# Moving a ring of matmul operands and the first loads of the down projection, in a two-layer encoder kernel

## The chip, the cores and the metric

One core of one Trainium2 chip runs the whole program. The metric is the device time of one execution in microseconds (us), the median of several executions. The engines are named as the profile names them: PE (TensorE matmuls), PEld (its weight loads), DVE (VectorE), ACT (ScalarE), POOL (GpSimd) and SP, which here only issues DMAs.

## The reference

Two layers, each a token mixer (first latent attention, then differential attention) and a SwiGLU feed-forward part, with a layer norm after each. The change touches the feed-forward part alone, which runs once in each layer:

```python
D_MODEL = 1024; SEQ = 1024; DEPTH = 2
D_FF = -(-8 * D_MODEL // (3 * 256)) * 256          # 2816
def _swiglu(x, w_gu, w_down):
    gate, up = jnp.split(x @ w_gu, 2, axis=-1)
    return (jax.nn.silu(gate) * up) @ w_down
...
h = _layernorm(ALPHA * h + _swiglu(h, ffn_w_gu[i], ffn_w_down[i]), ln_ffn_g[i], ln_ffn_b[i])
```

All data are float32.

## The kernel before, in words

**Precision.** A float32 product is made of three matmuls of rounded operands. `split` (L478) makes the two parts of an operand: the rounded high part `hi` is a cast on ACT (L480), the rest `lo` is a subtraction on DVE or POOL (L481). `op_unit` (L485) takes a place for such a pair from a ring of buffers: tags `wh` and `wl` have three places each, tag `o` has six.

**The gate and up stage** has 22 units of hidden columns. Each unit takes seven products of a Strassen-like scheme, called 1, 6, 2, 7, 5, 4, 3 in that order, each of 12 matmuls (`product`, L526). Their other operands are kept in SBUF: x itself, `t2` for product 6, `t3` for 7, `t1` for 5, `t4` for 4, `b22` for 3. `gr` is the raw weight tile of a unit; DVE makes its sums at L557 to L565 before the operands are split. DVE takes the products out of PSUM (L605 to L617), ACT does the silu (L628), DVE multiplies (L632, L633) into `hp`, POOL makes four further combinations `sh` of two units (L637 to L640), and SP stores both to `h_dr` in DRAM. The first two units of a layer have fewer products left, since part of them was made earlier; `stream` is the list of (unit, product) in which the products are asked for.

**The down stage** has seven passes of 11 units, each unit 12 matmuls (`step`, L795). The first pass, accumulator `dx`, multiplies `op_h_1_j` (from the loads `rh_1_0`, `rh_1_1`, `rh_1_2`, which hold units 0 to 3, 4 to 7 and 8 to 10 of `h_dr`) with `op_w_b_j` (printed in full `op_w_b11_j`, from the loads `tt_j` of the down weights). The second, `dy`, multiplies `op_h_5_j` with `op_w_t_j`, which is made from `tt_j` after its first half was replaced by a difference (the subtraction in `t1()`, L763). The `lo` parts of `op_h` are made on DVE, those of `op_w_b` on POOL, but on DVE for the first `early` units. The ring `o` of the down stage lies in the pool `fd`, which is opened where the gate stage's operands lay.

**Order.** A scheduler walks the program and its own costs and writes one order for each engine; `high_priority` and `behind(a, b)` (a stays behind b) steer it. On the chip each engine then runs its list strictly in order, so an instruction that waits holds back all that stands behind it on its engine. The same holds for SP's list of DMAs.

Of the kernel before, what the change touches and what calls it, by code (L numbers as in the profile page):

```python
# [16 lines left out]
P = 128  # L17
# [11 lines left out]
NFF = DFF // P  # L29
# [13 lines left out]
def trunk(  # L43
# [33 lines left out]
    V, A, G, T = nc.vector, nc.scalar, nc.gpsimd, nc.tensor  # L77
# [399 lines left out]

    def split(dst, src, eng):  # L478
        hi, lo = dst
        A.copy(hi, src)  # L480
        return eng.tensor_tensor(lo, src, f32(hi), ALU.subtract).ins  # L481

    turns = {"op": 0}

    def op_unit(src, eng, name, tags=("wh", "wl"), pool=None):  # L485

        tag = tags[turns["op"] % len(tags)]
        turns["op"] += 1
        where = wp if tag in ("wh", "wl") else pool
        t = where.tile([P, 2, 512], F32R, tag=tag, name=f"op_{name}", bufs=6 if pool is where else 3)  # L490
        turns["last"] = split((t[:, 0], t[:, 1]), src, eng)
        return t

    def swap(side):
        return "left" if side == "right" else "right"

    def ffn(side, xo, xst, pending, layer, x_src, x_dst, lng, lnb, next_x, spare=()):
# [5 lines left out]
        h_dr = [dr.tile([7, P, 4, 512], F32, name=f"h_dr{layer}_{g}") for g in range(3)]  # L503
        xst[2].close()
        st = ExitStack()
        pool = st.enter_context(tc.tile_pool(name=f"ff{layer}", bufs=1, side=side, reuse_waits="tile"))
        pool4 = st.enter_context(tc.tile_pool(name=f"ft{layer}", bufs=1, side=swap(side), reuse_waits="tile"))
        pool_a = xst[3]

# [2 lines left out]
        npre = 6  # L512
# [32 lines left out]
        begun = set()  # L545
# [79 lines left out]

        def activations(n, u2, u3, p1, g0):
            j, kh = n // 2, n % 2
            A.activation(u2, u2, AF.Silu)  # L628
            if kh == 0:
                hp[j] = big_tile(f"hp{layer}_{j}", F32).rearrange("p a (b c) -> p (a b) c", b=2)  # L630

            V.tensor_tensor(hp[j][:, kh], g0, p1, ALU.mult)  # L632
            V.tensor_tensor(hp[j][:, 3 - kh], u2, u3, ALU.mult)  # L633
            if kh:
                h11, h12, h22, h21 = (hp[j][:, i] for i in range(4))
                t = big_tile(f"sh{layer}_{j}", F32).rearrange("p a (b c) -> p (a b) c", b=2)
# [25 lines left out]

        r11, r12, r21, r22 = (xo["r", k, t] for k, t in ((0, 0), (0, 1), (1, 0), (1, 1)))
        xs = {}
        for key, where in (("t2", pool), ("t1", pool), ("b22", pool), ("t3", pool), ("t4", pool4)):
            xs[key] = [
                where.tile([P, 4, 512], F32R, tag=f"{key}{p}", name=f"{key}{p}_{nm}") for p in "hl"
            ]
# [1 line left out]
        def part(key, k, src, eng):  # L670
            split([t[:, k] for t in xs[key]], src[:, k], eng)

        stream = [(n, pr) for n in range(2) for pr in "53"]
        for n in range(NFF):
            stream += [(n, pr) for pr in ("674" if n < 2 else "67543" if n < npre else "1627543")]
        ahead = 4

        for k in range(4):
# [27 lines left out]
        for i in (1, 0):  # L706
            xst[i].close()
        st = ExitStack()
        pool = st.enter_context(tc.tile_pool(name=f"fd{layer}", bufs=1, side=side, reuse_waits="tile"))
        stx = ExitStack()  # L710
        poolh = stx.enter_context(tc.tile_pool(name=f"fh{layer}", bufs=2, side=swap(side), reuse_waits="tile"))
        poolx = stx.enter_context(tc.tile_pool(name=f"fx{layer}", bufs=1, side=swap(side), reuse_waits="tile"))
# [3 lines left out]
        tags = ("wh", "o", "wl", "o")  # L716

        tt = {
            j: poolx.tile([P, 2, 512], F32, tag=f"tt{j}", name=f"tt{layer}_{j}")
            for j in (range(11) if swap(side) == "left" else reversed(range(11)))  # L720
        }

        chain, in_order, banks_read = [], [], []

        def load_down(dst, src):

            i = nc.sync.dma_start(dst, src).ins
            if in_order:
                behind(i, chain[-1])
            chain.append(i)  # L730

        def from_h(s, name, tags=tags, late=False):

            for gi, (j0, j1) in enumerate(groups):
                r = poolh.tile([P, 4, 512], F32, tag="rawh", name=f"rh{layer}_{name}_{gi}")
                load_down(r[:, :j1 - j0], h_dr[gi][s, :, :j1 - j0, :])
                for j in range(j0, j1):
                    t = op_unit(r[:, j - j0], V, f"h{layer}_{name}_{j}", tags, pool)
                    if late and j > 1:
                        behind(turns["last"], banks_read[-1])  # L740
                    yield t

        def w_block(kh, cs, name):
# [6 lines left out]
                    yield r[:, j - j0]  # L750

        def unit(src, name, eng=G, tags=tags):
            return op_unit(src, eng, f"w{layer}_{name}", tags, pool)


        def b11():
            for j in range(11):
                load_down(tt[j], w_dn[layer, j].rearrange("p (b c) -> p b c", b=2))
                yield unit(tt[j][:, 0], f"b11_{j}", V if j < early else G)

        def t1():
# [18 lines left out]
        def t4():  # L780
            for j, r in enumerate(w_block(1, lo_half, "t4")):
                i = V.tensor_tensor(r, r, tt[j][:, 0], ALU.subtract).ins
                if j > 1:
                    behind(i, banks_read[-1])
                if next_x is not None:
                    yield unit(r, f"t4_{j}", G, ("o",))
                    continue
                t = poolx.tile([P, 2, 512], F32R, tag=f"tt{j}", name=f"wt4{layer}_{j}")
                split((t[:, 0], t[:, 1]), r, G)
                yield t  # L790

# [48 lines left out]
        hs = from_h(3, "5")  # L840
# [658 lines left out]
```

## Time and profile before

| quantity | value |
|---|---|
| median of 3 executions | 2296.66 us (2295.4 to 2297.1) |
| the profiled execution's own time | 2296.31 us |
| its span in the trace | 2294.4 us |
| PE busy | 2249.9 us, 98% of the span |
| DVE, ACT, POOL busy | 1562.8, 1017.9, 864.8 us |
| mean granted clock of PE | 0.995 of full speed |
| DMA moved | 288.28 MB, mean 126 GB/s |

PE is busy nearly all the time, so what counts are the short stretches in which it waits. The execution outside the span takes 2296.31 - 2294.4 = 1.9 us. The profile's waits name for each idle stretch of an engine the instruction that ended it; its timeline gives each instruction with its start.

### The profile page before, as it was taken

What the parts mean: (1) busy time and instruction counts of PE and PEld (TensorE: products, weight loads), DVE (VectorE), ACT (ScalarE), POOL (GpSimd) and SP (SyncE); (2) the same over time, 40 slices, a digit from 0 to 9 for tenths busy, and PEclk for the clock granted to TensorE, in tenths of its full rate; (3) what the DMA queues carried; (4) which work ended last, traced back from release to release, by engine and by line L of the source; (5) the groups of instructions that cost most, each with busy time, mean ns of one, the idle gap of its engine ahead of it and who ended that gap; (6) DMA issues with size and microseconds to landing.
All of it is one profiled execution on the core that took longest, in us unless ns stands there. A gap on an engine that the chain in (4) does not pass through costs nothing.

```text
span 2294.4 us, 31183 instructions
## 1 busy us (share of the span) xinstructions
PE 2249.9 (98%) x11410; PEld 1915.7 (83%) x11410; DVE 1562.8 (68%) x2899; ACT 1017.9 (44%) x2096; POOL 864.8 (38%) x688
## 2 busy tenths in 40 slices
PE   8999999999999999999999999999999999999997
PEld 8899997878888887888888888987778888887886
DVE  5667664696666668667476667676677666658777
ACT  4455573342333334445465656555432233324353
POOL 2232241114444445555432424221014444436564
PEclk9999999999999999999999999999999999999999
DMA  5010125334435338454310212054244232337353
GB/s 201 14 34 31 41 72 181 136 130 145 177 132 198 125 114 326 184 188 156 102 47 24 66 37 70 19 211 144 96 170 154 72 125 82 130 123 304 141 205 121
DMA packets 105545, 288.28 MB, mean 126 GB/s; under 512 B 7968, under 2 KB 30112, under 8 KB 94896
## 3 DMA queue, kind: packets, MB, share of 16 engines
q1 hardware_dynamic: 100976, 275.87, 33.6%
q0 software_dynamic: 4416, 10.42, 1.6%
q8 instruction: 90, 1.47, 0.3%
q14 instruction: 63, 0.52, 0.1%
HBM read 205.00 MB, written 77.07 MB: 123 GB/s over the span
## 4 chain that ended last, share of the span: by engine, by line
PE 88%; DVE 6%; DMA 3%; issue 2%; ACT 1%; POOL 1%; SPq 0%; DVEq 0%; POOLq 0%; ACTq 0%
PE gb L526 14%; PE gc L526 10%; PE ga L526 10%; PE dw L795 6%; PE zp_a L394 4%; PE s_a L216 4%; PE s_b L216 3%; PE dx L795 3%; PE dv L795 3%; PE bp L143 3%; PE bp L144 3%; PE bp L145 3%; PE dy L795 3%; PE o_a L255 2%; PE o_b L255 2%
## 5 line engine op out<-in xcount | busy, mean ns | idle before, releaser
L480 ACT CAST op_g<-gr 128x512 fp32r<-128x512 f32 x240 | 146.9, 621 | 370.8 <-PE gb L526 183.3
L481 POOL TENSOR_TENSOR op_g<-gr,op_g 128x512 fp32r<-128x512 f32 x104 | 146.4, 1413 | 248.2 <-ACT op_g L480 142.7
L481 DVE TENSOR_TENSOR op_h<-rh,op_h 128x512 fp32r<-128x512 f32 x154 | 163.8, 1091 | 63.4 <-ACT op_h L480 63.4
L526 PE MATMUL ga<-xh_m,op_g 128*128 128x512 f32 x512 | 168.1, 389 | 0.0
L480 ACT CAST op_h<-rh 128x512 fp32r<-128x512 f32 x154 | 92.9, 619 | 136.6 <-PE dx L795 36.1
L795 PE MATMUL dw<-op_w_t,op_h 128*128 128x512 f32 x660 | 151.4, 390 | 0.1
L795 PEld LDWEIGHTS dw<-op_w_t,op_h 128*128 128x128 f32 x660 | 123.6, 188 | 26.0 <-DVE op_h L481 0.5
L222 ACT ACTIVATE l_b<-l_b,mx_b 128x256 f32<-128x256 f32 (+7 forms) x128 | 99.5, 778 | 79.7 <-DVE mx_b L219 77.6
L1303 POOL TENSOR_SCALAR l_b<-l_b,r_b,cst 128x128 f32<-128x128 f32 (+3 forms) x64 | 52.8, 825 | 204.6 <-DVE r_b L224 194.0
L795 PE MATMUL dx<-op_w_b,op_h 128*128 128x512 f32 x528 | 122.2, 391 | 6.8 <-ACT op_w_b L480 3.9
L481 POOL TENSOR_TENSOR op_w_t<-tt,op_w_t 128x512 fp32r<-128x512 f32 x66 | 98.6, 1497 | 79.6 <-ACT op_w_t L480 77.8
L795 PEld LDWEIGHTS dx<-op_w_b,op_h 128*128 128x128 f32 x528 | 98.6, 188 | 30.1 <-ACT op_w_b L480 4.7
L481 DVE TENSOR_TENSOR op_g<-gr,op_g 128x512 fp32r<-128x512 f32 x136 | 110.8, 819 | 15.6 <-ACT op_g L480 15.3
L526 PE MATMUL gb<-t4h_f,op_g 128*128 128x512 f32 x352 | 115.9, 390 | 3.4 <-DVE tmp L609 3.4
L481 POOL TENSOR_TENSOR op_g<-s,op_g 128x512 fp32r<-128x512 f32 x40 | 54.3, 1358 | 167.9 <-ACT op_g L480 159.6
L526 PE MATMUL gb<-t2h_f,op_g 128*128 128x512 f32 x352 | 115.6, 390 | 0.4 <-DVE op_g L481 0.4
L526 PE MATMUL gc<-t1h_f,op_g 128*128 128x512 f32 x352 | 115.4, 389 | 0.0
L526 PE MATMUL gc<-b22h_f,op_g 128*128 128x512 f32 x352 | 115.3, 389 | 0.0
L526 PE MATMUL gb<-t3h_f,op_g 128*128 128x512 f32 x352 | 115.2, 389 | 0.0
L526 PEld LDWEIGHTS ga<-xh_m,op_g 128*128 128x128 f32 x512 | 96.1, 188 | 19.9
L143 PE MATMUL bp<-xT_f,h_wb 128*128 128x512 f32 x256 | 103.0, 402 | 0.0
L145 PE MATMUL bp<-xT_f,l_wb 128*128 128x512 f32 x256 | 101.6, 397 | 0.0
(378 smaller groups left out, 6753.9 us busy)
## 6 DMA issues: line engine op xcount, KB each, us to landing
gr<-in_w_gu SPq DMA_DIRECT2D x44, 1024.0 KB, 6.9
rh<-h_dr SPq DMA_DIRECT2D x28, 1024.0 KB, 4.8
h_dr<-sh SPq DMA_DIRECT2D x22, 1024.0 KB, 5.1
h_dr<-hp SPq DMA_DIRECT2D x22, 768.0 KB, 4.1
tt<-in_w_dn SPq DMA_DIRECT2D x22, 512.0 KB, 7.9
rh<-h_dr SPq DMA_DIRECT2D x14, 768.0 KB, 4.3
wo_dr<-op_pwo SPq DMA_DIRECT2D x16, 512.0 KB, 3.4
z<-xs_dr SPq DMA_DIRECT2D x16, 512.0 KB, 10.0
```

The costliest lines, as they stand in the source:

```text
L143: T.matmul(ps_out, lh, rh, start=(i == 0), stop=False)
L144: T.matmul(ps_out, lh, rl, start=False, stop=False)
L145: T.matmul(ps_out, ll, rh, start=False, stop=(i == n - 1))
L216: T.matmul(s[:, :w], lh, rh[:, ks], start=(j == 0), stop=(j == len(q_pass) - 1))
L222: A.activation(l[:, :n], l[:, :n], AF.Exp, bias=mx, scale=-1.0, accum_out=sm)
L255: T.matmul(po[:, c], a, b[:, j % 2, c], start=st, stop=sp_, skip_group_check=True)
L394: T.matmul(m, a[:, h, :], self.wo[h][w][:, c], start=(start and h == heads[0] and a is oh and w == 0), stop=(stop and h == heads[-1] and a ...
L480: A.copy(hi, src)
L481: return eng.tensor_tensor(lo, src, f32(hi), ALU.subtract).ins
L526: T.matmul(o, w[:, a, kc], x[b][:, k, :], start=(first and k == 0 and (a, b) == (0, 0)), stop=(k == 3 and a == 1), skip_group_check=True,)
L795: T.matmul(o, h[:, a, c], w[:, b_], start=(first and (a, b_) == (0, 0)), stop=(last and a == 1), skip_group_check=True,)
L1303: G.tensor_scalar(l1[:, :n], l1[:, :n], r1, nlam, ALU.mult, ALU.mult)
```

## The change

It does five things, in both layers.

- **Pools.** The gate stage's pool is cut in two (`t1`, `b22` in one, `t2`, `t3` in the other), and the down stage's pool too (results `z` and the norm's rows `g`, `b` in one, the ring `o` in the other), so that the ring `o` now lies under `t2` and `t3`, which the last gate unit reads earlier than `b22`. The tiles `tt` 0 to 3 get a pool apart from `tt` 4 to 10.
- **First four units of the down stage.** `early` goes from 3 to 4, h and w operands are asked for alternately, and the one load `rh_1_0` of 1 MB becomes four loads of 256 KB, one for each unit, put alternately with the loads of `tt_0` to `tt_3`.
- **`behind_gates`.** The casts of units 2 and 3 stay behind the last silu on ACT, and their subtractions behind the last `hp` product on DVE.
- **The subtractions of `t1()`.** That of unit j stays behind the `lo` part of `op_h_1_k`, k = min(j + 6, 10).
- **`stream`.** Products 6, 7 and 4 of the first two gate units alternate between the units: 6, 6, 7, 7, 4, 4.

```diff
     def split(dst, src, eng):
         hi, lo = dst
-        A.copy(hi, src)
+        turns["cast"] = A.copy(hi, src).ins
...
-        stream = [(n, pr) for n in range(2) for pr in "53"]
-        for n in range(NFF):
-            stream += [(n, pr) for pr in ("674" if n < 2 else "67543" if n < npre else "1627543")]
+
+        stream = [(n, pr) for n in range(2) for pr in "53"] + [(n, pr) for pr in "674" for n in range(2)]
+        for n in range(2, NFF):
+            stream += [(n, pr) for pr in ("67543" if n < npre else "1627543")]
...
-        for key, where in (("t2", pool), ("t1", pool), ("b22", pool), ("t3", pool), ("t4", pool4)):
+        for key, where in (("t1", pool), ("b22", pool), ("t2", pool2), ("t3", pool2), ("t4", pool4)):
...
-        pool = st.enter_context(tc.tile_pool(name=f"fd{layer}", bufs=1, side=side, reuse_waits="tile"))
+        pool, pool_o = [
+            st.enter_context(tc.tile_pool(name=f"f{n}{layer}", bufs=1, side=side, reuse_waits="tile")) for n in "do"
+        ]
...
+        def behind_gates():
+
+            behind(turns["cast"], turns["silu"])
+            behind(turns["last"], turns["hp"])
...
-                load_down(r[:, :j1 - j0], h_dr[gi][s, :, :j1 - j0, :])
+                one_by_one = name == "1" and gi == 0
+                if not one_by_one:
+                    load_down(r[:, :j1 - j0], h_dr[gi][s, :, :j1 - j0, :])
                 for j in range(j0, j1):
-                    t = op_unit(r[:, j - j0], V, f"h{layer}_{name}_{j}", tags, pool)
+                    if one_by_one:
+                        load_down(r[:, j - j0], h_dr[gi][s, :, j - j0, :])
+                    t = op_unit(r[:, j - j0], V, f"h{layer}_{name}_{j}", tags, pool_o)
                     if late and j > 1:
                         behind(turns["last"], banks_read[-1])
+                    if name == "1" and j > 1:
+                        behind_gates()
+                    splits.append(turns["last"])
                     yield t
...
-                V.tensor_tensor(tt[j][:, 0], tt[j][:, 1], tt[j][:, 0], ALU.subtract)
+                i = V.tensor_tensor(tt[j][:, 0], tt[j][:, 1], tt[j][:, 0], ALU.subtract).ins
+                behind(i, splits[min(j + 6, 10)])
...
-        early = 3
...
         with tc.high_priority(100):
-            hs, ws = (itertools.chain([next(x) for _ in range(early)], x) for x in (hs, ws))
+            begun = [[next(x) for x in (hs, ws)] for _ in range(early)]
+        hs, ws = (itertools.chain(b, x) for b, x in zip(zip(*begun), (hs, ws)))
```

The amount of work on PE, DVE and ACT hardly changes; the places change. Three of them follow, of layer 0. Lines of the changed kernel are shifted: its L560, L562, L564, L568, L608, L610, L612, L614 are L557, L559, L561, L565, L605, L607, L609, L611 of before; L738 is L727, L789 is L763, L645 and L646 are L642 and L643.

**First gate units, DVE.** `tmp_0` and `tmp_1` collect the products of units 0 and 1, and the L609 row reads product 7 of unit 0 out of PSUM (`gb_0`). Before:

```order
L605 TENSOR_TENSOR tmp_0_5697<-pg_0_5315,gb_0_5696 128x512
L481 TENSOR_TENSOR op_g_2_6_5734<-gr_2_5575,op_g_2_6_5734 128x512
L607 TENSOR_TENSOR tmp_0_5697<-tmp_0_5697,gc_05_5628 128x512
L557 TENSOR_TENSOR gr_4_5730<-gr_4_5730 128x512
L607 TENSOR_TENSOR tmp_0_5697<-tmp_0_5697,gc_03_5646 128x512
L605 TENSOR_TENSOR tmp_1_5760<-pg_0_5315,gb_1_5759 128x512
L559 TENSOR_TENSOR gr_4_5730<-gr_4_5730 128x512
L607 TENSOR_TENSOR tmp_1_5760<-tmp_1_5760,gc_15_5662 128x512
L561 TENSOR_TENSOR gr_4_5730<-gr_4_5730 128x512
L565 TENSOR_TENSOR s_0_4_5954<-gr_4_5730 128x512
L607 TENSOR_TENSOR tmp_1_5760<-tmp_1_5760,gc_13_5678 128x512
L609 TENSOR_TENSOR tmp_0_5697<-pg_0_5315,gb_0_5696 128x512
```

The same place in the changed kernel:

```order
L608 TENSOR_TENSOR tmp_0_5700<-pg_0_5318,gb_0_5699 128x512
L560 TENSOR_TENSOR gr_3_5601<-gr_3_5601 128x512
L481 TENSOR_TENSOR op_g_2_6_5740<-gr_2_5578,op_g_2_6_5740 128x512
L610 TENSOR_TENSOR tmp_0_5700<-tmp_0_5700,gc_05_5631 128x512
L562 TENSOR_TENSOR gr_3_5601<-gr_3_5601 128x512
L610 TENSOR_TENSOR tmp_0_5700<-tmp_0_5700,gc_03_5647 128x512
L608 TENSOR_TENSOR tmp_1_5720<-pg_0_5318,gb_1_5719 128x512
L568 TENSOR_TENSOR s_0_3_5862<-gr_3_5601 128x512
L564 TENSOR_TENSOR gr_3_5601<-gr_3_5601 128x512
L560 TENSOR_TENSOR gr_4_5736<-gr_4_5736 128x512
L610 TENSOR_TENSOR tmp_1_5720<-tmp_1_5720,gc_15_5665 128x512
L612 TENSOR_TENSOR tmp_0_5700<-pg_0_5318,gb_0_5699 128x512
```

Ten rows stand between the first and the last in both. The four on `gr_4`, of which the first needs a load, were among them, and now only the first of these is; three on `gr_3` have come in. In layer 1 no row on `gr_3` comes in and the last two on `gr_4` go behind the L612 row, so that eight are left. On PE, product 4 of unit 0, which writes the same PSUM bank `gb_0`, has two matmuls of unit 2 ahead of it that stood behind it before, in both layers.

**End of the gate stage, PE.** `gc_215` is product 3 of the last unit, the one that reads `b22`; `dx` is the first pass of the down stage. Before:

```order
L526 MATMUL gb_21_8271<-t4h_f_5485,op_g_21_4_8268 128x512
L526 MATMUL gc_215_8315<-b22h_f_5481,op_g_21_3_8286 128x512
...
L526 MATMUL gc_215_8315<-b22h_f_5481,op_g_21_3_8286 128x512
L795 MATMUL dx_0_8416<-op_w_b_0_8405,op_h_1_0_8395 128x512
L795 MATMUL dx_1_8417<-op_w_b_0_8405,op_h_1_0_8395 128x512
```

In the changed kernel:

```order
L529 MATMUL gb_21_8274<-t4h_f_5488,op_g_21_4_8271 128x512
L822 MATMUL dx_0_8436<-op_w_b_0_8409,op_h_1_0_8405 128x512
...
L822 MATMUL dx_3_8439<-op_w_b_0_8409,op_h_1_0_8405 128x512
L529 MATMUL gc_215_8318<-b22h_f_5482,op_g_21_3_8289 128x512
...
L529 MATMUL gc_215_8318<-b22h_f_5482,op_g_21_3_8289 128x512
L822 MATMUL dx_3_8439<-op_w_b_0_8409,op_h_1_0_8405 128x512
L822 MATMUL dx_0_8436<-op_w_b_1_8417,op_h_1_1_8413 128x512 x3
```

Eleven of the twelve matmuls of down unit 0 now run ahead of the last gate product (12 matmuls). In layer 1 unit 0 stands around product 4, and the first two matmuls of unit 1 ahead of the last gate product too. On SP the loads of unit 0 to 3 now stand in pairs, and those of `tt_3` and `rh_1_1` ahead of the store of the last `hp`; the load of the last three h units, `rh_1_2`, stands behind the same stores and the same eleven `tt` loads as before, and now directly behind the store of `sh_10`, which stood ahead of `tt_8` to `tt_10`.

**DVE at the eighth h unit.** `op_h_1_8` is the first of the three units of `rh_1_2`; the L763 rows (L789 in the changed kernel) are the subtractions of `t1()`; `op_h_5_0` is the first operand of pass `dy`. Before:

```order
L763 TENSOR_TENSOR tt_8_8380<-tt_8_8380 128x512
L763 TENSOR_TENSOR tt_9_8379<-tt_9_8379 128x512
L763 TENSOR_TENSOR tt_10_8378<-tt_10_8378 128x512
L481 TENSOR_TENSOR op_h_1_8_8559<-rh_1_2_8557,op_h_1_8_8559 128x512
L481 TENSOR_TENSOR op_h_1_9_8578<-rh_1_2_8557,op_h_1_9_8578 128x512
L481 TENSOR_TENSOR op_h_1_10_8597<-rh_1_2_8557,op_h_1_10_8597 128x512
L481 TENSOR_TENSOR op_h_5_0_8626<-rh_5_0_8624,op_h_5_0_8626 128x512
```

In the changed kernel:

```order
L789 TENSOR_TENSOR tt_1_8397<-tt_1_8397 128x512
L481 TENSOR_TENSOR op_h_1_8_8572<-rh_1_2_8570,op_h_1_8_8572 128x512
L789 TENSOR_TENSOR tt_2_8396<-tt_2_8396 128x512
L481 TENSOR_TENSOR op_h_1_9_8591<-rh_1_2_8570,op_h_1_9_8591 128x512
L789 TENSOR_TENSOR tt_3_8395<-tt_3_8395 128x512
L481 TENSOR_TENSOR op_h_1_10_8610<-rh_1_2_8570,op_h_1_10_8610 128x512
L789 TENSOR_TENSOR tt_4_8394<-tt_4_8394 128x512
...
L789 TENSOR_TENSOR tt_10_8388<-tt_10_8388 128x512
L481 TENSOR_TENSOR op_h_5_0_8639<-rh_5_0_8637,op_h_5_0_8639 128x512
```

Before, all eleven subtractions stood ahead of `op_h_1_8`, and three rows led from it to `op_h_5_0`. Now only two of them (tt_0, tt_1) stand ahead, and from `op_h_1_8` to `op_h_5_0` there are twelve rows to go: nine subtractions, `op_h_1_9`, `op_h_1_10` and `op_h_5_0` itself. Earlier on the same engine the four rows `op_h_1_2`, `op_w_b_2`, `op_h_1_3` and `op_w_b_3` now follow directly on the last `hp` product; the last of the four was POOL's.

## Rows read from the trace of the kernel before

**Rows 1.** The page, busy time, share of the span and instructions.

```profile
PE 2249.9 (98%) x11410; PEld 1915.7 (83%) x11410; DVE 1562.8 (68%) x2899; ACT 1017.9 (44%) x2096; POOL 864.8 (38%) x688
```

**Rows 2.** Waits of PE: line, releaser, us in total, times, longest us.

```profile
PE dx L795 <- ACT op_w_b L480: 3.9, 2, 1.9
PE gb L526 <- DVE tmp L609: 3.4, 3, 1.4
...
PE dx L795 <- DVE op_w_b L481: 1.8, 3, 1.2
PE dx L795 <- DVE op_h L481: 1.0, 1, 1.0
```

**Rows 3.** Timeline of PE, first gate units of both layers: start us, duration us.

```profile
504.01 0.39 PE L526 MATMUL gb<-t3h_f,op_g 128*128 128x512 f32 x1
505.80 0.50 PE L526 MATMUL gb<-t4h_f,op_g 128*128 128x512 f32 x1 [1.40 <-DVE tmp L609]
...
1700.15 0.50 PE L526 MATMUL gb<-t4h_f,op_g 128*128 128x512 f32 x1 [1.36 <-DVE tmp L609]
```

**Rows 4.** Timeline of DVE, first gate units of both layers.

```profile
498.88 0.69 DVE L557 TENSOR_TENSOR gr<-gr 128x512 f32<-128x512 f32 x1 [0.61 <-DMA gr<-in_w_gu]
...
505.07 0.67 DVE L609 TENSOR_TENSOR tmp<-pg,gb 128x512 f32<-128x512 f32 x1
...
1697.12 1.78 DVE L565 TENSOR_TENSOR s<-gr 128x512 f32<-128x512 f32 x1
```

**Rows 5.** Timeline of PE from gate to down stage, layer 0.

```profile
871.37 0.39 PE L526 MATMUL gc<-b22h_f,op_g 128*128 128x512 f32 x1
873.71 3.94 PE L795 MATMUL dx<-op_w_b,op_h 128*128 128x512 f32 x16 [1.95 <-ACT op_w_b L480]
877.94 20.67 PE L795 MATMUL dx<-op_w_b,op_h 128*128 128x512 f32 x88 [0.29 <-DVE op_w_b L481]
899.62 6.66 PE L795 MATMUL dx<-op_w_b,op_h 128*128 128x512 f32 x28 [1.02 <-DVE op_h L481]
906.12 20.11 PE L795 MATMUL dy<-op_w_t,op_h 128*128 128x512 f32 x88
```

**Rows 6.** Timeline of PE, the same in layer 1.

```profile
2067.85 3.96 PE L795 MATMUL dx<-op_w_b,op_h 128*128 128x512 f32 x16 [1.95 <-ACT op_w_b L480]
...
2100.05 4.24 PE L795 MATMUL dy<-op_w_t,op_h 128*128 128x512 f32 x18
```

**Rows 7.** Timeline of DVE, first pass of the down stage, layer 0.

```profile
873.18 0.69 DVE L633 TENSOR_TENSOR hp<-tmp 128x512 f32<-128x512 f32 x1
...
889.81 1.28 DVE L763 TENSOR_TENSOR tt<-tt 128x512 f32<-128x512 f32 x2
892.70 5.17 DVE L763 TENSOR_TENSOR tt<-tt 128x512 f32<-128x512 f32 x3 [1.60 <-POOL op_w_b L481]
897.79 8.67 DVE L481 TENSOR_TENSOR op_h<-rh,op_h 128x512 fp32r<-128x512 f32 x7
```

**Rows 8.** Timeline of POOL, the same stretch.

```profile
873.96 1.68 POOL L637 TENSOR_TENSOR sh<-hp 128x512 f32<-128x512 f32 x1 [9.13 <-DVE hp L633]
...
895.58 5.13 POOL L481 TENSOR_TENSOR op_w_t<-tt,op_w_t 128x512 fp32r<-128x512 f32 x3
```

**Rows 9.** Timeline of ACT: casts of the eighth to tenth h unit.

```profile
894.97 1.66 ACT L480 CAST op_h<-rh 128x512 fp32r<-128x512 f32 x3
```

**Rows 10.** Timeline of SP's queue, both layers: first issue, time to the last issue's end.

```profile
873.90 0.38 SPq L642 DMA_DIRECT2D h_dr<-hp  x1
...
881.13 9.12 SPq L727 DMA_DIRECT2D rh<-h_dr  x2
...
2054.11 1.28 SPq L727 DMA_DIRECT2D tt<-in_w_dn  x3
```

**Rows 11.** The tile rh from 855 to 895 us: issue to landing.

```profile
DMA to landing us min/median/max: 4.8/7.3/13.8
```

**Rows 12.** Windows: PE, PEld, DVE, ACT, POOL busy, clock, DMA share, GB/s.

```profile
885.00:890.00 5.00, 5.00 (x24) 4.14 (x23) 5.00 (x5) 0.83 (x2) 3.74 (x3) 1.00 1.09 411
```

More of the change, by code (lines that the diff above doesn't have):

```diff
@@ L505, in ffn @@
         st = ExitStack()
-        pool = st.enter_context(tc.tile_pool(name=f"ff{layer}", bufs=1, side=side, reuse_waits="tile"))
+        pool, pool2 = [
+            st.enter_context(tc.tile_pool(name=f"f{n}{layer}", bufs=1, side=side, reuse_waits="tile")) for n in "fg"
+        ]
         pool4 = st.enter_context(tc.tile_pool(name=f"ft{layer}", bufs=1, side=swap(side), reuse_waits="tile"))
@@ L627, in activations @@
             j, kh = n // 2, n % 2
-            A.activation(u2, u2, AF.Silu)
+            turns["silu"] = A.activation(u2, u2, AF.Silu).ins
             if kh == 0:
@@ L632, in activations @@
             V.tensor_tensor(hp[j][:, kh], g0, p1, ALU.mult)
-            V.tensor_tensor(hp[j][:, 3 - kh], u2, u3, ALU.mult)
+            turns["hp"] = V.tensor_tensor(hp[j][:, 3 - kh], u2, u3, ALU.mult).ins
             if kh:
@@ L708, in ffn @@
         st = ExitStack()
-        pool = st.enter_context(tc.tile_pool(name=f"fd{layer}", bufs=1, side=side, reuse_waits="tile"))
+        pool, pool_o = [
+            st.enter_context(tc.tile_pool(name=f"f{n}{layer}", bufs=1, side=side, reuse_waits="tile")) for n in "do"
+        ]
         stx = ExitStack()
         poolh = stx.enter_context(tc.tile_pool(name=f"fh{layer}", bufs=2, side=swap(side), reuse_waits="tile"))
-        poolx = stx.enter_context(tc.tile_pool(name=f"fx{layer}", bufs=1, side=swap(side), reuse_waits="tile"))
+        pool_w, poolx = [
+            stx.enter_context(tc.tile_pool(name=f"f{n}{layer}", bufs=1, side=swap(side), reuse_waits="tile"))
+            for n in "wx"
+        ]
         z, sums = {}, {}
@@ L716, in ffn @@
         tags = ("wh", "o", "wl", "o")
+        early = 4
+        place = [pool_w] * early + [poolx] * (11 - early)
         tt = {
-            j: poolx.tile([P, 2, 512], F32, tag=f"tt{j}", name=f"tt{layer}_{j}")
+            j: place[j].tile([P, 2, 512], F32, tag=f"tt{j}", name=f"tt{layer}_{j}")
             for j in (range(11) if swap(side) == "left" else reversed(range(11)))
         }
-        chain, in_order, banks_read = [], [], []
+        chain, in_order, banks_read, splits = [], [], [], []
         def load_down(dst, src):
@@ L752, in unit @@
         def unit(src, name, eng=G, tags=tags):
-            return op_unit(src, eng, f"w{layer}_{name}", tags, pool)
+            return op_unit(src, eng, f"w{layer}_{name}", tags, pool_o)
         def b11():
@@ L758, in b11 @@
                 load_down(tt[j], w_dn[layer, j].rearrange("p (b c) -> p b c", b=2))
-                yield unit(tt[j][:, 0], f"b11_{j}", V if j < early else G)
+                t = unit(tt[j][:, 0], f"b11_{j}", V if j < early else G)
+                if 1 < j < early:
+                    behind_gates()
+                yield t
         def t1():
             for j in range(11):
-                V.tensor_tensor(tt[j][:, 0], tt[j][:, 1], tt[j][:, 0], ALU.subtract)
+                i = V.tensor_tensor(tt[j][:, 0], tt[j][:, 1], tt[j][:, 0], ALU.subtract).ins
+                behind(i, splits[min(j + 6, 10)])
                 yield unit(tt[j][:, 0], f"t1_{j}")
@@ L787, in t4 @@
                     continue
-                t = poolx.tile([P, 2, 512], F32R, tag=f"tt{j}", name=f"wt4{layer}_{j}")
+                t = place[j].tile([P, 2, 512], F32R, tag=f"tt{j}", name=f"wt4{layer}_{j}")
                 split((t[:, 0], t[:, 1]), r, G)
```

## The prediction

> **What bounds the kernel now.** I read the page first. PE is busy 98% of the span [rows 1], so a change that adds no matmul can only win what PE waits, or lose by new waits. So the second view is the list of PE's waits. Of its lines four belong to what the change moves [rows 2]: 3.9 us before `dx` for a cast on ACT, 3.4 us before a gate product for L609 on DVE, 1.8 us and 1.0 us before `dx` for subtractions on DVE. That is 10.1 us in both layers, and it is all that could be won if nothing new came. Third, the timeline of PE at these places.
>
> At the first gate units PE stands still 1.40 us in layer 0 and 1.36 us in layer 1, both times for the L609 row on DVE, which has to empty the PSUM bank that product 4 writes next [rows 3]. In layer 0 that row starts only at 505.07, after a string of DVE work on raw weights, one piece of which waited 0.61 us for a load [rows 4]. The third wait for L609, 3.4 - 1.40 - 1.36 = 0.64 us, is at the end of layer 1's gate stage.
>
> At the end of the gate stage of layer 0 the last gate matmul starts at 871.37 and `dx` at 873.71, after 1.95 us of waiting; pass `dy` begins at 906.12 [rows 5]. A matmul takes (20.11 - 0.16) / 88 = 0.2267 us from start to start (the row of 88 [rows 5]; 0.16 is the tail of the last), a unit of 12 takes 2.72 and the pass of 132 29.92. From 873.71 - 1.95 = 871.76 to 906.12 are 34.36 us, so 4.4 us are lost in this pass. In layer 1 it is 2100.05 - (2067.85 - 1.95) - 29.92 = 4.2 us [rows 6], and the 0.64 us just named.
>
> What stands behind the waits is read from the other engines. The last `hp` product on DVE is at 873.18 [rows 7], POOL then starts `sh` at 873.96 [rows 8], and SP, which held back everything behind it, issues the store of `hp` at 873.90 [rows 10]. From then on the DMA engines are full: in 885 to 890 us their share is 1.09 at 411 GB/s [rows 12]. `rh_1_2` is issued at 881.13 [rows 10] and takes 13.8 us, the longest landing of that tile [rows 11], so it is there at 894.9, and ACT casts the eighth h unit at 894.97 [rows 9]. Lastly DVE: a subtraction takes 1.28 / 2 = 0.64 us at 889.81, but 5.17 / 3 = 1.72 us at 892.70, when POOL works too, and 8.67 / 7 = 1.24 us over the mixed stretch from 897.79 [rows 7].
>
> **The first gate units.** In layer 0 ten DVE rows stand ahead of the L609 row, as before, but a load is no longer waited for early among them: the row ends 0.61 us sooner. Two matmuls that now stand ahead of product 4 give 2 x 0.2267 = 0.45 us more. Of 1.40 us 1.06 go for sure and at most all; I take 1.2. In layer 1 two of the ten rows go behind L609, one of 0.64 and one of 1.78 us [rows 4, 7]; these 2.4 us are more than the 1.36. Sum: -1.2 - 1.36 = **-2.55 us**. Its bounds are 0, if another row takes the place, and -2.76. The rows moved behind have about a unit's time there, since the next product 4 comes 2.72 us later.
>
> **The new ring and the pairs of loads.** Operands of down unit 0 no longer wait for `b22` and for the casts behind the silu. So unit 0 starts where product 3 started, one unit before its old end, and the 1.95 us go, and with them the small waits for w operands that follow (0.29 us [rows 5]), and in layer 1 the 0.64 us. All 4.4 and 4.8 us would go if nothing were late next. Three things are.
>
> First, product 3, whose last matmul had its place from 871.37 to 871.60 [rows 5], ends 2.72 us later, at 874.3, and `hp`, POOL's `sh` and the store follow at the same distance: `hp` at 875.9, `sh` from 876.7 to 881.8. On DVE `op_h_1_2`, `op_w_b_2`, `op_h_1_3`, `op_w_b_3` follow directly behind `hp`, from 876.5. PE comes to unit 2 one unit of product 3's end, at 877.05, and wants the `lo` of w at its fifth matmul, 0.9 us later. Alone the four take 4 x 0.64 = 2.6 us and all are in time. At 1.72 the second ends at 879.9, 2.0 us late, after which the fourth is hardly late. With the first half alone: between 0 and 2.0, I take **1.2**. The last of the four was POOL's; POOL has `sh` to make then, which gains nothing from that.
>
> Second, `rh_1_2`. All the loads that came ahead of it still do, the DMA engines are as full, and the store of `hp` comes up to 2.72 us later. PE would come to unit 8 six units after unit 2 and the 1.2 us: 877.05 + 16.32 + 1.2 = 894.6. If the load lands as before, the cast ends at 894.97 + 0.55 = 895.5 (1.66 / 3 each [rows 9]), 0.9 us late; if it lands 2.72 us later, 3.6 late. Since the engines have work in between, nearer the first: **1.5**. The rows of norm weights, which now load a little earlier, and the split of `rh_1_0` lie within these ends, and what is loaded for units 0 to 3 has several us of cover.
>
> Third, the twelve DVE rows from `op_h_1_8` to `op_h_5_0`. The `lo` of unit 8 is done at about 896.8. Pass `dy` would start at 894.6 + 1.5 + 3 x 2.72 = 904.3 and wants the `lo` of `op_h_5_0` 0.9 us later, at 905.2. Twelve rows at 0.64 end at 904.5: no wait. At the mixed 1.24 they end at 911.7: 6.5 us. POOL's unbroken work lasted to 900.7 [rows 8] and will last somewhat longer, so three or four rows at 1.72 and the rest at 0.64: 10.9 or 12.0 us, 2.5 or 3.6 late. I take **3.0**. Before, eleven of these subtractions were done while DVE waited for `rh_1_2` anyway; now DVE stands idle there. In front of the z additions, which follow, there is a whole pass of cover.
>
> So layer 0 loses 1.2 + 1.5 + 3.0 = 5.7 us instead of 4.4: **+1.3**. In layer 1 the `tt` loads go out at 2054.11 only [rows 10], when product 1 has freed their place, and the loads of units 1 to 3 stand behind the first of them; for that I add 0.3: 6.0 instead of 4.8, **+1.2**. From below each layer comes to 2.1 us (no wait at units 2 and 3, so that unit 8 is reached 1.2 us sooner and waits 0.9 + 1.2, and none at `dy`), from above to 2.0 + 3.6 + 6.5 = 12.1.
>
> **Sum.** -2.55 + 1.3 + 1.2 = -0.05 us against the execution's own 2296.31: 2296.3 us. That execution is 0.35 us under the median of 2296.66, which is well inside the three runs. I forecast 2296.3.
>
> **A rule to weigh.** The loads run in a stretch where the DMA engines give 411 GB/s [rows 12], though the `tt` loads there have only 512 KB each; at that rate a quarter of `rh_1_0` (0.26 MB) costs 0.64 us, and the four as much as the one. The Trainium skill, page "DMA: Bandwidth & Descriptors", asks in its section "Bandwidth" for loads of 1 MiB or more, and gives about 2 us of fixed cost for each in "Anatomy of one DMA"; by it, an estimate, the three additional loads cost 6 us in each layer if nothing overlaps, and the sum would be up to 12 us higher. The trace speaks against it: the engines stay full there with loads of half that size, since several are under way.
>
> **Rivals.** (A) *Faster.* DVE isn't held by POOL: no wait at units 2 and 3, none at `dy`. PE then reaches unit 8 at 893.4, and `rh_1_2` is awaited for 2.1 us (0.9 + 1.2), perhaps 2.7. A loss of 2.4 instead of 4.4 and 2.7 instead of 4.8 gives -4.1, with the gates -6.7: **2289.6**. For it speaks the row at 889.81; against it POOL's row from 895.58 [rows 7, 8].
>
> (B) *Slower.* The twelve rows run at the mixed 1.24: 3.5 us more per layer, **2303.3**. It decides from a wait of 3.0 + 2.3 = 5.3 us, which is (905.2 + 5.3 - 896.8) / 12 = 1.14 us for each row. For it speaks the row from 897.79, with the same engine mix; against it, that POOL soon has to wait for free places of the ring.
>
> (C) *The transfers are the limit anyway.* PE waits as long as before for `rh_1_2`, and nothing else is late: the boundary changes nothing, only the gates count: **2293.8**.
>
> (D) *Small loads.* The shortest `rh` load took 4.8 us [rows 11], of which 1.05 MB at 411 GB/s are 2.55; if the other 2.25 us aren't covered for the three additional loads, `rh_1_2` lands 6.75 us later, and with it unit 8 and all behind it, in each layer: 2296.3 + 13.5 = **2309.8**. The page of the Trainium skill just named would have it so. For it speaks nothing in the rows but that landing; against it the full engines of [rows 12].
>
> **How the numbers follow.** About 0.2% of the time, 4.6 us, is what a measurement can tell from no change. Chances: the forecast, with its sizes up to 3 us off, 0.60; A 0.20; B 0.09; C 0.08; D 0.03. Faster by over 0.2% is A, 0.20; within 0.2% the forecast and C, 0.68; slower B and D, 0.12. The range reaches down to A's price and up to where B begins to cost both layers: 2289.3 to 2301.0, and leaves out half of A and nearly all of B and D, 0.2. The likeliest case alone would be 2293.3 to 2299.3.
>
> **What would show it.** At the first gate units no wait for L609 of more than 0.3 us. `dx` in layer 0 starts at 868.9 without a wait. The waits of `dx` for DVE at units 2 and 3 come to about 1.2 us; PE then waits at unit 8 for the cast of `op_h_1_8`, about 1.5 us, and `dy` for `op_h_5_0` on DVE, about 3 us. DVE should show several us of idle time before `op_h_1_8`. The prediction is wrong if this DVE line isn't late (then A), if its rows take over 1.14 us each (then B), or if the order of arrival of the loads differs from what their queue suggests.

## The result, and the profile after

The changed kernel took 2299.91 us (median of 14 executions), the kernel before 2295.34 us on the same chip: a ratio of 1.0019, with a 95% interval from 1.0012 to 1.0027. It is 4.6 us slower. The forecast was no difference (-0.05 us in the sum); the time lies within the range that was given, but the slowdown was not foreseen. The profiled execution is the slowest of the 14, at 2302.95 us, 3.0 us above the median.

First the page and PE's waits (line, releaser, us in total, times, longest), beside [rows 1] and [rows 2]:

```profile
PE 2254.2 (98%) x11410; PEld 1918.4 (83%) x11410; DVE 1547.0 (67%) x2901; ACT 1016.8 (44%) x2096; POOL 865.8 (38%) x686
...
PE dy L822 <- DVE op_h L481: 4.1, 2, 2.1
PE dx L822 <- ACT op_h L480: 2.6, 2, 1.5
PE dx L822 <- DVE op_w_b L481: 2.1, 4, 0.8
...
PE dx L822 <- ACT op_w_b L480: 1.9, 3, 1.2
PE gb L529 <- DVE tmp L612: 1.1, 2, 0.7
```

PE has the same 11410 matmuls and is busy 4.3 us longer, which waits can't explain; more on that below. The waits of the boundary have new names: the 3.9 us for the first cast of a w operand are down to 1.9, but `op_h` at unit 8 and above all `dy`, which didn't wait at all, have come in.

PE's timeline in layer 0, beside [rows 5]:

```profile
865.55 0.47 PE L529 MATMUL gb<-t4h_f,op_g 128*128 128x512 f32 x1 [0.72 <-DVE tmp L612]
868.36 2.66 PE L822 MATMUL dx<-op_w_b,op_h 128*128 128x512 f32 x11
...
878.21 3.04 PE L822 MATMUL dx<-op_w_b,op_h 128*128 128x512 f32 x12 [0.62 <-DVE op_w_b L481]
881.61 12.99 PE L822 MATMUL dx<-op_w_b,op_h 128*128 128x512 f32 x56 [0.36 <-DVE op_w_b L481]
896.09 8.45 PE L822 MATMUL dx<-op_w_b,op_h 128*128 128x512 f32 x36 [1.49 <-ACT op_h L480]
904.38 1.97 PE L822 MATMUL dy<-op_w_t,op_h 128*128 128x512 f32 x8
908.43 21.87 PE L822 MATMUL dy<-op_w_t,op_h 128*128 128x512 f32 x95 [2.07 <-DVE op_h L481]
```

Unit 0 runs ahead of product 3 without a wait; units 2 and 3, unit 8 and `dy` wait, as listed in the prediction. New is the 0.72 us at product 4. DVE in the same layer, beside [rows 7]:

```profile
864.12 0.69 DVE L481 TENSOR_TENSOR op_h<-rh,op_h 128x512 fp32r<-128x512 f32 x1 [5.33 <-ACT op_h L480]
864.73 0.68 DVE L612 TENSOR_TENSOR tmp<-tmp,gb 128x512 f32<-128x512 f32 x1
...
896.07 0.69 DVE L481 TENSOR_TENSOR op_h<-rh,op_h 128x512 fp32r<-128x512 f32 x1 [6.51 <-ACT op_h L480]
...
900.20 7.58 DVE L789 TENSOR_TENSOR tt<-tt 128x512 f32<-128x512 f32 x7
907.70 2.48 DVE L481 TENSOR_TENSOR op_h<-rh,op_h 128x512 fp32r<-128x512 f32 x4
```

DVE stands idle 6.51 us until `rh_1_2` is cast, and then has seven subtractions in a row (7.58 us) ahead of `op_h_5_0`, while PE waits. The first two rows explain the 0.72 us: L612, for which product 4 waits, stands behind the `lo` part of `op_h_1_0`, and that behind its cast on ACT, which starts only at 863.47, when the load of `rh` has landed.

Layer 1, PE, beside [rows 6]:

```profile
2060.21 1.21 PE L822 MATMUL dx<-op_w_b,op_h 128*128 128x512 f32 x4 [1.15 <-ACT op_w_b L480]
...
2079.70 1.19 PE L822 MATMUL dx<-op_w_b,op_h 128*128 128x512 f32 x4 [0.56 <-ACT op_w_b L480]
2081.18 10.31 PE L822 MATMUL dx<-op_w_b,op_h 128*128 128x512 f32 x44 [0.29 <-POOL op_w_b L481]
2092.64 8.45 PE L822 MATMUL dx<-op_w_b,op_h 128*128 128x512 f32 x36 [1.15 <-ACT op_h L480]
...
2104.98 7.29 PE L822 MATMUL dy<-op_w_t,op_h 128*128 128x512 f32 x24 [2.07 <-DVE op_h L481]
```

Here are three waits more than in layer 0 (unit 0, unit 4 twice), and the last row is odd: 24 matmuls take 7.29 us, where 24 x 0.2267 + 0.16 = 5.6. The window behind it (columns as in [rows 12]) says why:

```profile
2105.00:2110.00 5.00, 5.00 (x15) 4.05 (x16) 5.00 (x9) 0.62 (x1) 1.29 (x1) 0.67 0.42 158
```

PE is busy all 5 us and does 15 matmuls instead of 22: its granted clock is 0.67 in the mean, that is 1.2 GHz for two thirds of the window and 2.4 GHz for the rest. The record of the clock shows the lower level for 3.41 us from 2104.9 on, as PE starts again after its wait; it costs half of that, 1.7 us. A second such stretch, 3.41 us from 2275.6 on in the last pass, is in this execution too; together the two make most of the 4.3 us that PE is busy longer.

To see where the time goes I match each matmul with the same one of the trace before (same tiles, same number) and take by how much it starts later. The table has the growth of this from one place to the next. These are single executions: with the same edit the first gates of layer 1 range from -0.43 to -2.25, and one execution is 2.7 us behind the one before already ahead of the first gates, where nothing was edited. So differences of about 1 us in this table say little.

| kernel | first gates, layer 0 | boundary, layer 0 | first gates, layer 1 | boundary, layer 1 | lower clock at a boundary |
|---|---|---|---|---|---|
| changed | -1.75 | +2.15 | -1.13 | +5.27 | layer 1, 3.41 us |
| gates alone | -1.63 | -0.23 | -1.71 | +0.69 | none |
| all subtractions ahead of unit 8 | -1.67 | +6.61 | -0.54 | +5.92 | both, 6.83 and 3.41 us |
| norm rows early | -1.65 | +1.78 | -2.25 | +3.94 | layer 1, 3.41 us |
| one load | -1.62 | +1.63 | -0.91 | +0.91 | layer 0, 3.41 us |
| order of subtractions alone | -0.05 | +3.69 | -0.39 | +0.95 | layer 0, 3.41 us |
| subtractions spread | -1.71 | -0.26 | -1.97 | +1.22 | none |
| one load, spread | -1.63 | -2.46 | -1.05 | -1.38 | none |
| the same, norm rows early | -1.74 | -0.09 | -1.29 | -2.79 | layer 0, 3.41 us |
| spread, product 3 first | -1.78 | -1.69 | -0.72 | -0.98 | none |
| one load, spread, ring back | -1.61 | -2.13 | -0.43 | -2.01 | none |

### The profile page after: what moved, and what is told of

It is laid out like the page before. It is cut to its first block, busy times and chain, and to the rows that moved or that the text cites. A ratio compares the mean times of both kernels' runs of the same rounds, so it can differ in the third digit from the quotient of the medians.

```text
span 2301.2 us, 31204 instructions
## 1 busy us (share of the span) xinstructions
PE 2254.2 (98%) x11410; PEld 1918.4 (83%) x11410; DVE 1547.0 (67%) x2901; ACT 1016.8 (44%) x2096; POOL 865.8 (38%) x686
## 4 chain that ended last, share of the span: by engine, by line
PE 87%; DVE 5%; DMA 4%; issue 2%; ACT 1%; POOL 1%; SPq 0%; DVEq 0%; POOLq 0%; ACTq 0%
PE gb L529 15%; PE ga L529 10%; PE gc L529 10%; PE dw L822 5%; PE zp_a L394 4%; PE s_a L216 4%; PE s_b L216 3%; PE dv L822 3%; PE bp L143 3%; PE bp L144 3%; PE bp L145 3%; PE dy L822 2%; PE o_a L255 2%; PE o_b L255 2%; PE dx L822 2%
## 5 line engine op out<-in xcount | busy, mean ns | idle before, releaser
L481 DVE TENSOR_TENSOR op_h<-rh,op_h 128x512 fp32r<-128x512 f32 x154 | 156.7, 1044 | 86.6 <-ACT op_h L480 86.6
```

## The experiments

Each ratio is against the kernel before, with its 95% interval. The kernel before itself measured 2295.0, 2295.7 or 2296.1 us beside the experiments, so a difference between two of their medians can be off by 1 us for that alone.

**Gates alone** (kernel before with one edit).

```diff
-        stream = [(n, pr) for n in range(2) for pr in "53"]
-        for n in range(NFF):
+        stream = [(n, pr) for n in range(2) for pr in "53"] + [(n, pr) for pr in "674" for n in range(2)]
+        for n in range(2, NFF):
```

> The kernel before with the new order of products 6, 7, 4 for the first two gate units, and nothing else. Theory (the loss sits wholly at the boundary between gate and down stage): the two waits for L609 shrink as in the changed kernel, where the matmuls behind them ran 1.75 us (layer 0) and 1.13 us (layer 1) earlier against the kernel before; nothing later takes it back: about 2.9 us faster than before. Rival (the time won at the gates is lost again before the boundary, since the boundary waits for transfers that don't come sooner): no difference, within 1 us.

Measured: 2291.93 us, ratio 0.9987 (0.9979 to 0.9996), 3.1 us faster than before. The theory holds: the gain at the gates is real and stays. So everything else in the change costs about 8 us (2299.9 - 2291.9 by the medians, 4.6 + 3.1 against the kernel before).

**All subtractions ahead of unit 8** (changed kernel).

```diff
-                behind(i, splits[min(j + 6, 10)])
+                behind(i, splits[min(j + 6, 7)])
```

> The changed kernel with the subtractions of t1() kept behind op_h_1_7 at the latest (min(j + 6, 7)), so that on DVE all eleven stand ahead of op_h_1_8, in the 6.5 and 11 us in which DVE otherwise stands idle for rh_1_2. Theory (the line of nine subtractions ahead of op_h_5_0 is one main loss): both waits of 2.07 us at the start of dy go, and the 3.4 us at half clock that followed the one of layer 1: 4 to 6 us less than the changed kernel, about 2295. Rival (the later store of hp and the late rh_1_2 are what sets the pass): the subtractions now work against POOL's op_w_b, and PE waits for those instead: the changed kernel's time within 1 us.

Measured: 2305.27 us, ratio 1.0043 (1.0030 to 1.0057). My theory as I put it fell for the time, and the rival's outcome is exceeded: it is 5 us slower than the changed kernel. DVE, then PE:

```profile
890.25 13.74 DVE L789 TENSOR_TENSOR tt<-tt 128x512 f32<-128x512 f32 x10
...
904.64 8.98 PE L822 MATMUL dx<-op_w_b,op_h 128*128 128x512 f32 x28 [3.81 <-DVE op_h L481]
```

Ten subtractions take 13.74 us, 1.37 each, while POOL works on `op_w_b` and `op_w_t` (886.6 to 901.6 us with hardly a break); alone they take 0.64 [rows 7]. The Trainium skill, page "SBUF — State Buffer", section "Who interferes with whom", says that DVE and GpSimd share a pair of SBUF ports as an exclusive lock; the durations here agree. The wait at `dy` went, as the theory had it, and one of 3.81 us (2.75 in layer 1) came at unit 8; around it the clock falls, in both layers.

**Norm rows early** (changed kernel; in layer 1 `g` and `b` are made ahead of the tiles `z`, so that they lie elsewhere).

```diff
+        if layer:
+            g = bcast_row(pool, lng, D, f"fg{layer}", "g")
+            b = bcast_row(pool, lnb, D, f"fb{layer}", "b")
         for tb in range(4):
             z[tb] = pool.tile([P, D], F32, tag="zd", name=f"z{layer}_{tb}", bufs=4)
...
-        g = bcast_row(pool, lng, D, f"fg{layer}", "g")
-        b = bcast_row(pool, lnb, D, f"fb{layer}", "b")
+        if layer == 0:
+            g = bcast_row(pool, lng, D, f"fg{layer}", "g")
+            b = bcast_row(pool, lnb, D, f"fb{layer}", "b")
```

> The changed kernel, where in layer 1 the rows g and b of the norm are the first tiles of their pool and not the last, so that they no longer lie under b22, which is read last. Theory (in layer 1 the 1 MB of these rows moved from 2059 to 2069 us, behind the lull of the DMA engines, and pushes hp, tt_4 and rh_1_2 back): their loads go out ahead of the lull again, rh_1_2 lands about 2.5 us sooner (1 MB at 419 GB/s), the waits at units 4 and 8 of layer 1 (0.56, 0.29, 1.15 us) go: about 2 us less than the changed kernel, about 2298. Rival (rh_1_2 is late because hp is stored late and SP stands behind it): rh_1_2 lands as late and the time is the same within 0.5 us at these places.

Measured: 2298.94 us, ratio 1.0018 (1.0008 to 1.0028). In the time this can't be told from the changed kernel; in the trace the mechanism is plain. POOL's queue in layer 1, of the kernel before and of the changed kernel:

```profile
2059.37 0.61 POOL L152 DMA_DIRECT2D fg<-in_ln_ffn_g  x1 [6.77 <-PE gb L526]
...
2069.23 0.61 POOL L152 DMA_DIRECT2D fg<-in_ln_ffn_g  x1 [17.10 <-PE gc L529]
```

and of this one, followed by its PE:

```profile
2059.29 0.61 POOL L152 DMA_DIRECT2D fg<-in_ln_ffn_g  x1 [6.78 <-PE gb L529]
...
2091.04 8.45 PE L822 MATMUL dx<-op_w_b,op_h 128*128 128x512 f32 x36 [0.35 <-ACT op_h L480]
...
2103.97 8.27 PE L822 MATMUL dy<-op_w_t,op_h 128*128 128x512 f32 x28 [2.66 <-DVE op_h L481]
```

The loads go out 10 us sooner, unit 4's waits are gone, unit 8 waits 0.35 instead of 1.15 us; but `dy`'s wait grows to 2.66 us. What is won at unit 8 is lost at `dy` in good part; DVE's line of nine subtractions is the same.

**One load** (changed kernel).

```diff
-                one_by_one = name == "1" and gi == 0
+                one_by_one = False
```

> The changed kernel with rh_1_0 as one load of 1 MB again, ahead of the tt loads. The scheduler then puts product 3 (b22) ahead of down unit 0, as in the kernel before. Theory (the split makes op_h_1_1 wait behind tt_0, and ACT's and DVE's lists behind op_h): the waits of 0.72 us at product 4 in layer 0 and 1.15 us at unit 0 in layer 1 go, hp and what hangs on it come 2.7 us sooner, so that unit 8's waits shrink too: 2 to 4 us less than the changed kernel, 2296 to 2298. Rival (loads one by one are what lets unit 0 run ahead of product 3, and that covers the silu): PE waits at units 1 to 3 for DVE about as much as it wins, within 1 us of the changed kernel.

Measured: 2294.40 us, ratio 0.9998 (0.9989 to 1.0006), 5.5 us less than the changed kernel, more than expected. In layer 0 product 4 and units 0 to 2 don't wait at all, with product 3 in its old place; in layer 1 the wait at unit 0 is gone, and product 4 waits 0.65 us instead, as in the kernel before. `dy` still waits, 2.44 and 2.06 us.

**The order of the subtractions alone** (kernel before, with the list `splits` of the change and these two lines).

```diff
-                V.tensor_tensor(tt[j][:, 0], tt[j][:, 1], tt[j][:, 0], ALU.subtract)
+                i = V.tensor_tensor(tt[j][:, 0], tt[j][:, 1], tt[j][:, 0], ALU.subtract).ins
+                behind(i, splits[min(j + 6, 10)])
```

> The kernel before with one part of the change alone: the subtraction of t1() for unit j stays behind op_h_1_k, k = min(j + 6, 10). Nothing else is moved. Theory (nine subtractions between op_h_1_8 and op_h_5_0 make dy wait whatever else is changed): a new wait of 2 to 3 us at the start of dy in each layer, against at most 1.2 us won at unit 2 and 1.0 us at unit 8; a stretch at half clock behind it where it comes: 2 to 6 us slower than before. Rival (DVE's line is late only because the changed kernel's rh_1_2 and hp are late): no wait at dy, same or up to 2 us faster than before.

Measured: 2301.27 us, ratio 1.0023 (1.0014 to 1.0032): 5.6 us slower than before, by this part alone. PE in both layers, and the window behind the first wait:

```profile
873.40 30.50 PE L797 MATMUL dx<-op_w_b,op_h 128*128 128x512 f32 x132 [1.95 <-ACT op_w_b L480]
909.52 6.69 PE L797 MATMUL dy<-op_w_t,op_h 128*128 128x512 f32 x21 [3.81 <-DVE op_h L481]
...
2105.72 8.46 PE L797 MATMUL dy<-op_w_t,op_h 128*128 128x512 f32 x36 [2.79 <-DVE op_h L481]
...
910.00:915.00 5.00, 5.00 (x17) 3.92 (x16) 5.00 (x10) 0.62 (x1) 1.28 (x1) 0.66 0.46 157
```

The whole pass `dx` runs its 132 matmuls without a break, so this order does help there; but `dy` waits 3.81 and 2.79 us, and in layer 0 the clock falls behind that.

**Subtractions spread** (changed kernel).

```diff
-                behind(i, splits[min(j + 6, 10)])
+                behind(i, splits[min(j + 6, 7) if j < 5 else j + 6])
```

> The changed kernel with the subtractions of t1() spread: those of units 0 to 4 stay behind op_h_1_7 at the latest, that of unit j from 5 on behind op_h_5_(j-5), so that only three rows lead from op_h_1_8 to op_h_5_0. Theory (what counts is how many subtractions DVE has to do in a stretch where PE is waiting, not their sum): the waits of 2.07 us at dy go, the 3.8 us wait of the experiment with all of them ahead of unit 8 doesn't come since three fewer us of work stand there, and without a long wait no half clock: 3 to 6 us less than the changed kernel, about 2295. Rival (DVE and POOL together are full in this pass, so the work is late wherever it stands): the wait moves on to t1's own units in dy, same time as the changed kernel within 1 us.

Measured: 2293.35 us, ratio 0.9990 (0.9981 to 0.9999), 6.6 us less than the changed kernel. `dy` doesn't wait in either layer, unit 8 waits 1.65 and 1.27 us. Layer 0:

```profile
895.44 8.45 PE L822 MATMUL dx<-op_w_b,op_h 128*128 128x512 f32 x36 [1.65 <-ACT op_h L480]
903.73 11.50 PE L822 MATMUL dy<-op_w_t,op_h 128*128 128x512 f32 x50
```

The theory holds, the rival falls: the work of DVE and POOL fits, if it stands in the right stretches.

**One load and spread**, both edits.

> rh_1_0 as one load and the subtractions spread, the rest as in the changed kernel. Theory: the gains of both add, since one acts ahead of unit 8 and the other at dy: about 4 us less than with one load alone (2294.4), so about 2290. Rival (DVE and POOL together are full): as with one load alone, 2294 within 1 us.

Measured: 2289.27 us, ratio 0.9972 (0.9963 to 0.9981). The gains add for the most part: 10.6 us less than the changed kernel, of 5.5 and 6.6 us singly. PE in layer 0:

```profile
869.57 9.23 PE L822 MATMUL dx<-op_w_b,op_h 128*128 128x512 f32 x40
878.96 13.00 PE L822 MATMUL dx<-op_w_b,op_h 128*128 128x512 f32 x56 [0.16 <-DVE op_w_b L481]
893.24 8.46 PE L822 MATMUL dx<-op_w_b,op_h 128*128 128x512 f32 x36 [1.27 <-ACT op_h L480]
901.54 10.82 PE L822 MATMUL dy<-op_w_t,op_h 128*128 128x512 f32 x47
```

All that is left there is 0.16 us and unit 8's wait for its load; in layer 1 there are 0.65 us at product 4, 0.45 and 0.37 at unit 4 and 1.27 at unit 8.

**The same with the norm rows early.**

> As the kernel with one load and the subtractions spread, and in layer 1 the rows g and b of the norm as the first tiles of their pool. Theory: in layer 1 they load before the lull, rh_1_2 lands 1 to 2.5 us sooner and unit 8's wait shrinks by about 1 us: about 2289. Rival: SP's place behind the store of hp sets the landing: no difference to the kernel without it.

Measured: 2287.53 us, ratio 0.9968 (0.9957 to 0.9979): the lowest median here, 8 us under the kernel before, but its distance from the one without is within the intervals. The theory's mechanism is not borne out: in layer 1 unit 8 waits 1.27 us as without it; what went are the two waits at unit 4.

**Spread, product 3 first** (split loads, PE's order held by hand).

```diff
-                    T.matmul(
+                    turns["gate"] = T.matmul(
...
-                    )
+                    ).ins
...
+                if first and (a, b_) == (0, 0) and "gate" in turns:
+                    behind(i, turns["gate"])
...
```

> The kernel with the subtractions spread (loads of units 0 to 3 split as in the changed kernel), in which PE keeps product 3 of the last gate unit ahead of down unit 0, as it is with one load. It tells the two things apart that came with the one load: the load itself, and product 3's place. Theory (product 3 one unit later is what hurts: hp, sh, tt_4 and rh_1_2 come 2.7 us later, and units 2 and 3 wait for DVE): most of the 4.1 us between the spread kernel with split loads (2293.4) and with one load (2289.3) is won, 2289 to 2291. Rival (the split loads hurt: op_h_1_1 waits behind tt_0, ACT's and DVE's lists behind it): the waits of 0.7 us at product 4 in layer 0 and 1 us in layer 1 stay and little is won, 2292.5 to 2294.

Measured: 2291.65 us, ratio 0.9981 (0.9972 to 0.9990). Between the two theories: of the 4.1 us that one load is worth, about half comes with product 3's place and half with the load itself (1.7 and 2.4 by the medians; by the ratios against the kernel before the halves are equal). The waits at product 4 stay, 0.62 us in layer 0 and 2.00 in layer 1, as the rival said; those of units 2 and 3 are gone, as the theory said. The distances are about as wide as the intervals.

**One load, spread, ring back** (pools of the gate operands and of the ring as in the kernel before).

```diff
-        for key, where in (("t1", pool), ("b22", pool), ("t2", pool2), ("t3", pool2), ("t4", pool4)):
+        for key, where in (("t2", pool), ("t1", pool), ("b22", pool), ("t3", pool), ("t4", pool4)):
...
-        pool, pool_o = [
-            st.enter_context(tc.tile_pool(name=f"f{n}{layer}", bufs=1, side=side, reuse_waits="tile")) for n in "do"
-        ]
+        pool = st.enter_context(tc.tile_pool(name=f"fd{layer}", bufs=1, side=side, reuse_waits="tile"))
...
```

> The kernel with one load and the subtractions spread, but the ring o and the gate operands back in one pool each, as in the kernel before (t2, t1, b22, t3 in this order; ring o under t1 and b22). Theory (the ring's place is what lets the operands of units 0 and 1 be made before b22 is read): a wait of about 2 us before dx comes back in each layer, 2292.5 to 2293.5 against 2289.3. Rival (as product 3 runs ahead of unit 0 anyway, the ring's place matters no more): 2289 to 2290.

Measured: 2288.68 us, ratio 0.9967 (0.9955 to 0.9980). The rival holds: without the ring's new place the kernel is as fast. It shows in a wait of 0.48 us at unit 0 in each layer (in layer 1 the waits at unit 4 are gone in return); layer 0:

```profile
869.00 1.07 PE L818 MATMUL dx<-op_w_b,op_h 128*128 128x512 f32 x4
870.54 21.19 PE L818 MATMUL dx<-op_w_b,op_h 128*128 128x512 f32 x92 [0.48 <-DVE op_w_b L481]
```

## Why the prediction was wrong

**The gates: right.** -2.55 us forecast, -3.1 measured with that part alone. In layer 1 of the changed kernel 0.38 us of the wait for L612 are left (1699.95), a little more than the 0.3 us that the prediction allowed.

**Units 2 and 3, unit 8: right.** 1.2 and 1.5 us forecast for layer 0; 0.62 + 0.36 and 1.49 measured, with the releasers named.

**The line of subtractions: right in mechanism, in part mis-sized.** 3.0 us forecast, 2.07 measured in each layer. PE does eight matmuls of `dy` without the `lo` of `op_h_5_0`, not four, which is 0.9 us. It is the largest single loss: alone it costs 5.6 us, and spreading it wins 6.6.

**Layer 0: right after `dx` begins, in part by luck, and a miss ahead of it.** From unit 0's start at 868.36 to the start of `dy`, its wait counted in (908.43 - 8 x 0.2267 = 906.62), are 38.26 us, for 144 matmuls of 32.64: 5.6 us lost, forecast 5.7. That they agree so well is in part luck: counted from start to start of the matmuls, units 2 and 3 lost 1.5 us and not 1.2, unit 8 1.8 and not 1.5, and `dy` 2.2 and not 3.0. The step that failed is ahead of it: "the 1.95 us go" was right, but nothing was looked for at product 4, where 0.72 us came anew. The gain was read from PE's order, and DVE's, in which L612 slid behind a row that waits for a load, was not read at that place.

**Layer 1: the step that failed.** For it the prediction added 0.3 us to layer 0's figures. From where PE begins to wait for unit 0 to the start of `dy`, its wait counted in, it loses 2104.98 - 8 x 0.2267 - (2060.21 - 1.15) - 156 x 0.2267 = 8.7 us, against 6.0 forecast. From start to start units 0 and 1 lost 1.5 us and unit 4 1.4, for which the prediction had those 0.3 us in all; units 2 and 3 lost 1.8, unit 8 1.5 and `dy` 2.2. Two things are behind the waits that were not forecast. The norm's rows, said to "load a little earlier", do so in layer 0 alone; in layer 1 the pools are laid out from the other side, the rows lie under `b22`, and 1 MB moves from 2059 to 2069 us, ahead of the store of `hp` and of `tt_4`. The trace of the experiment shows both ends of it. And `op_h_1_1` waits for its quarter of the load, which stands behind `tt_0`, with the cast of `op_w_b_0` behind it on ACT: 1.15 us at unit 0. ACT in layer 1 of the changed kernel:

```profile
2059.02 0.62 ACT L480 CAST op_h<-rh 128x512 fp32r<-128x512 f32 x1 [4.26 <-DMA rh<-h_dr]
2059.54 0.61 ACT L480 CAST op_w_b<-tt 128x512 fp32r<-128x512 f32 x1
```

`tt_0`, issued at 2053.65, was there after 3.8 us, at 2057.4; the quarter, issued at 2054.04, took 5.0 us. So the cast of `op_w_b_0` stood ready for 2.1 us behind the cast of `op_h_1_1`. With the whole load the wait is gone.

**The clock: not in the prediction.** 1.7 us in the profiled execution at the boundary, behind the very wait that was forecast.

**The sum of it.** -2.9 us at the gates, +2.15 and +5.27 at the boundaries (1.7 of it the clock) make +4.5 us. That this is nearly the 4.6 us between the medians is chance: the two profiled executions lie 6.8 us apart, and the other 2.3 us are 0.8 us of small differences elsewhere and 1.5 us at the second stretch of the lower clock, in the last pass. How often either stretch occurs in the 14 executions is not known. By medians alone, the gates win 3.1 us and the rest costs about 8, where +2.5 was forecast.

Rival B came as near as the forecast (3.4 us off against 3.6), but by other terms: its twelve rows were to make `dy` wait over 5.3 us, and it waited 2.07. Rival D's mechanism isn't what happened: `rh_1_2` landed 13.7 us after its issue at 881.70, 0.5 us later than before and not 6.75, and while the quarters were loaded the DMA engines' share was 1.02 and 0.98 (865 to 875 us), against 1.00 and 0.95 before. That one load is faster all the same has other reasons, above.

Not tested apart are `behind_gates`, the fourth early unit and the pool of `tt` 0 to 3; the ring's place was tested only with the whole load.

## What to carry to other kernels

When a change reorders an in-order engine, walk its list once for each wait that is to go and read what now stands ahead of the instruction that ends it; the row that waits for a load is the one to look for. Work that an engine can do while it waits anyway should neither all go ahead of the next urgent operand nor all behind it: give each such row the place from which its own reader needs it. And do the sum for every copy of a stage, since two layers with mirrored buffers wait for different things.

## What the runs showed of the hardware

PE's granted clock can fall to its lower level around a wait. In these traces ten waits of PE at `dx` or `dy` took 2.06 to 3.81 us, and at six of them the record shows 1.2 GHz for 3.41 or 6.83 us, beginning between 1.8 us before the wait's end and 1.3 us after it; in layer 1 of the changed kernel 24 matmuls then took 7.29 us in place of 5.6. Of the seven waits of 1.84 and 1.95 us there, only the one of 1.84 was followed by it. The length of the wait alone doesn't decide. The two of 2.07 us in the changed kernel differ: the one of layer 0 has no such stretch, the one of layer 1 has it. And elsewhere in the same twelve traces PE waits once 1.92 us for `l_b` (in the changed kernel until 1558.30), and in eight of them the lower clock begins within 1.3 us of the end of that wait, in four not. What decides is open; no run here sets it apart. A wait of about 2 us can thus cost nearly twice its length, as in layer 1 of the changed kernel: 2.07 us and 1.7 us more.
